# A one-core decoder trunk: second operand of the opening between two quarters of x, last k tile's weights ahead of its columns and split

## The chip, the cores and the metric

The kernel runs on one core of a Trainium2 chip. The metric is device time in microseconds (us), the median of several executions; lower is better. The engines are named as the profile names them: PE (matmul; PEld is its weight load), DVE (vector), ACT (scalar), POOL, and SP, whose queue issues most of the transfers.

## The reference, cut to what matters

Two residual layers over x (256 tokens by 2048), each a mixer and a SwiGLU feed-forward. Every sub-layer first normalises x and modulates it with a shift and a scale that are products of silu(c) with a large matrix:

```python
silu_c = jax.nn.silu(c)
for layer in range(DEPTH):
    mod = silu_c @ mod_w[layer] + mod_b[layer]
    sh1, sc1, g1, sh2, sc2, g2 = jnp.split(mod, 6, axis=-1)
    h = modulate(rms_norm(x, norm_mix_gain[layer]), sh1, sc1)
    ...                                  # proj = h @ w_in, first step of the mixer
```

For the opening this means: before the first projection can use row block k of `w_in` (128 of the 2048 inner values, a "k tile", 16 of them), the 128 shifts and 128 scales of that block must be known, and each takes a full row of `mod_w`: two tiles of 128x2048, 1 MB each.

## The kernel before, in words

The opening (`start`) works by k tiles, kt = 0 to 15. For each one SP fetches three 1 MB tiles: two of `mod_w` (`mod_s`, here called the columns of kt, `fetch_columns`) and one of the projection's first 2048 output columns (`raw_s`, its weights, `fetch_weights`). All 48 go through SP's one queue, in program order: an issue that waits for a buffer holds up all issues behind it. `rawp` has three buffers for weights (`RAWS`), so weights kt wait until weights kt-3 have been read.

- `columns(kt)`: DVE multiplies each of the two column tiles with `silu_c` and sums (`mod_sum`, L109), then two small operations (`column_factors`, L998 and L1000) make scale and shift.
- `operand(kt)`: ACT applies them to the turned x (`tm_s`, L1015), casts to fp32r (`hT_s` high part, L1016), and DVE makes the low part (L1017).
- `weights(kt)`: unless kt is in `PLAIN`, ACT casts the weights to a high part (`hi_s`, L167, two halves) and DVE subtracts to a low part (`lo_s`, L169, two halves).
- `products(kt)`: PE adds this k tile to eight accumulators of 128x512 (four groups of columns in the order 1, 3, 0, 2, two tiles of tokens). A split tile takes three fp32r matmuls for each (L1031 high by high, L1032 high by low weights, L1033 low by high), 24 in all; a plain tile takes one fp32 matmul for each (L1026), which the trace lists as two entries, 16 in all.

The loop body for kt issues the columns of kt+2, the weights of kt+1, then `columns(kt + 1)`, `weights(kt)`, `operand(kt + 1)` and `products(kt)`: on DVE the split of tile kt stands behind the sums of tile kt+1. Every instruction in `start` keeps its written order (`manual_schedule`). Ahead of the loop x itself is scaled and turned in four quarters of 512 columns (`scaled`, `turned`), and tile 0 is multiplied in two halves.

After the opening ACT reads accumulators 1 and 3 through SiLU into `qg_A` (L1113) and PE starts on the next projection pieces (`acc_A`, L190 to L192), whose accumulator is one that `qg_A` frees. The rest of the program is placed by a scheduler.

Of the kernel before, what the change touches and what calls it, by code (L numbers as in the profile page):

```python
# [18 lines left out]
KT = D // P  # L19
# [2 lines left out]
LOG_MIN_FORGET = float(np.log(np.float32(1e-30)))  # L22
LEVELS = (64, 32, 16, 8, 4, 2, 1)
FFN_GROUPS = ((0, 6), (6, 12), (12, 18), (18, 22))
PLAIN = (0, 3, 6, 9, 12, 15)
LOOKAHEAD = 2
RAWS = 3
HIS = 4
# [38 lines left out]
def build(tc, ctx, a, out):  # L67
# [9 lines left out]
    def ps_mix(name):  # L77
        return env["pm"].tile([P, 512], F32, tag="pm", name=name)

    def h_tile(name):  # L80
        return hpool.tile([P, 2, 4, T], F32R, tag="h", name=name)
# [26 lines left out]
    def mod_sum(tile, l, part, j):  # L108
        nc.vector.scalar_tensor_tensor(tile, tile, 1.0, silu_c, ALU.mult, ALU.mult,  # L109
                                       accum_out=modc[l, part][:, j:j + 1])  # L110
# [169 lines left out]
    def rsqrt(dst, ss, n, width, name, between=lambda: None):  # L280

        m = small.tile([P, width], F32, tag=f"rs_m{width}", name=f"rsm_{name}")
        u = small.tile([P, width], F32, tag=f"rs_u{width}", name=f"rsu_{name}")
        nc.vector.tensor_scalar(m, ss, 1.0 / n, EPS, ALU.mult, ALU.add)
        nc.scalar.activation(u, m, AF.Ln)
        nc.scalar.activation(dst, u, AF.Exp, scale=-0.5)
        between()
        nc.vector.scalar_tensor_tensor(u, dst, -0.5, dst, ALU.mult, ALU.mult)
        nc.vector.tensor_tensor(u, u, m, ALU.mult)
        nc.vector.scalar_tensor_tensor(dst, u, 1.5, dst, ALU.add, ALU.mult)  # L290
# [26 lines left out]
    def new_ss(name):  # L317
        return small.tile([P, 2, 4], F32, tag="ss", name=f"ss_{name}")
# [643 lines left out]
    def start():  # L962
# [13 lines left out]
        hT, raw_w, raw_m = [], {}, {}  # L976

        def fetch_columns(kt):
            for part in (1, 0):
                if (2 * kt + 1 - part) % 3 == 2:  # L980
                    tl = rawp.tile([P, D], F32, tag="modraw", name=f"mod_s{part}_{kt}", bufs=2)
                else:
                    tl = hpool.tile([P, D], F32, tag="h", name=f"mod_s{part}_{kt}")
                nc.sync.dma_start(out=tl, in_=a["mod_w"][0, part * KT + kt])
                raw_m[part, kt] = tl

        def fetch_weights(kt):
            raw_w[kt] = rawp.tile([P, 2048], F32, tag="raw", name=f"raw_s{kt}")
            nc.sync.dma_start(out=raw_w[kt], in_=a["start_w"][kt])

        def columns(kt):
            for part in (1, 0):
                mod_sum(raw_m[part, kt], 0, part, kt)
            column_factors(kt)

        def column_factors(kt):
            k = slice(kt, kt + 1)
            nc.vector.scalar_tensor_tensor(acol[:, k], modc[0, 1][:, k], b1[:, k], cols[:, C_NMIX + kt:C_NMIX + kt + 1],  # L998
                                           ALU.add, ALU.mult)
            nc.vector.tensor_tensor(modc[0, 0][:, k], modc[0, 0][:, k], cols[:, C_MODB + kt:C_MODB + kt + 1], ALU.add)  # L1000

        def weights(kt):
            if kt in PLAIN:
                return None
            return [split_weights(raw_w[kt][:, n * 1024:(n + 1) * 1024], f"s{kt}_{n}") for n in range(2)]
# [3 lines left out]
        def operand(kt):  # L1009
            if kt % 4 == 0:  # L1010
                hT.append(h_tile(f"hT_s{kt // 4}"))
            h = hT[-1]
            k = slice(kt, kt + 1)
            tm = tms[kt] = pool.tile([P, T], F32, tag="tm", name=f"tm_s{kt}", bufs=3)
            nc.scalar.activation(tm, xT[:, kt, :], AF.Identity, bias=modc[0, 0][:, k], scale=acol[:, k])  # L1015
            nc.scalar.copy(out=h[:, 0, kt % 4], in_=tm)  # L1016
            nc.vector.tensor_tensor(h[:, 1, kt % 4], tm, h[:, 0, kt % 4], ALU.subtract)  # L1017

        def products(kt, ws, ns):

            for n in ns:
                sl = slice((n % 2) * 512, (n % 2 + 1) * 512)
                for t in range(2):
                    o = acc[n][t]
                    if ws is None:
                        nc.tensor.matmul(o, tms[kt][:, t * P:(t + 1) * P], raw_w[kt][:, n * 512:(n + 1) * 512],  # L1026
                                         start=(kt == 0), stop=(kt == KT - 1))
                        continue
                    hi, lo = ws[n // 2]
                    a_hi, a_lo = act(kt, t)  # L1030
                    nc.tensor.matmul(o, a_hi, hi[:, sl], start=(kt == 0), stop=False)  # L1031
                    nc.tensor.matmul(o, a_hi, lo[:, sl], start=False, stop=False)  # L1032
                    nc.tensor.matmul(o, a_lo, hi[:, sl], start=False, stop=(kt == KT - 1))  # L1033

        def scaled(nb, t, engine):
            if engine is nc.scalar:
                nc.scalar.activation(xt[nb][:, t], xt[nb][:, t], AF.Copy, scale=r[:, t:t + 1])
            else:
                nc.vector.tensor_scalar(xt[nb][:, t], xt[nb][:, t], r[:, t:t + 1], None, ALU.mult)

        def turned(nb):
            for half in range(2):
                ps = ps_mix(f"xT_{nb}_{half}")
                for kk in range(2):
                    for t in range(2):
                        c0 = (half * 2 + kk) * P
                        nc.tensor.transpose(ps[:, kk * T + t * P:kk * T + (t + 1) * P], xt[nb][:, t, c0:c0 + P], ident)
                k0 = nb * 4 + half * 2
                nc.scalar.copy(out=xT[:, k0:k0 + 2, :].rearrange("p k t -> p (k t)"), in_=ps)

        fetch_columns(0)
        fetch_weights(0)
        fetch_columns(1)
        act = act_of(hT)
# [5 lines left out]
        with tc.tile_pool(name="ps_t", bufs=4, space=PSUM) as pt:  # L1060
            env["pm"] = pt
            ss = new_ss("s")
            nc.vector.tensor_scalar(b1, cols[:, C_MODB + KT:C_MODB + 2 * KT], 1.0, None, ALU.add)
            for nb in range(4):
                ps = ps_mix(f"c_{nb}")
                sl = slice(nb * 512, (nb + 1) * 512)
                nc.tensor.matmul(ps, ones, c_row[:, sl], start=True, stop=True)
                nc.scalar.activation(silu_c[:, sl], ps, AF.Silu)
                junk = [pool.tile([P, 512], F32, tag=f"junk{t}", name=f"junk_s{nb}{t}", bufs=1) for t in range(2)]
                nc.vector.scalar_tensor_tensor(junk[0], xt[nb][:, 0], 1.0, xt[nb][:, 0], ALU.mult, ALU.mult,  # L1070
                                               accum_out=ss[:, 0, nb:nb + 1])
                nc.scalar.activation(junk[1], xt[nb][:, 1], AF.Square, accum_out=ss[:, 1, nb:nb + 1])
            nc.scalar.preload_act_table_set(EXP_LN)
            tot = small.tile([P, 2], F32, tag="sst2", name="sst_s", bufs=1)
            r = small.tile([P, 2], F32, tag="rstd2", name="rstd_s", bufs=1)
            nc.vector.tensor_reduce(tot, ss, op=ALU.add, axis=AX.X)
            rsqrt(r, tot, D, 2, "s", lambda: mod_sum(raw_m[1, 0], 0, 1, 0))
            for t in range(2):
                scaled(0, t, nc.vector)
            turned(0)  # L1080
            mod_sum(raw_m[0, 0], 0, 0, 0)
            column_factors(0)
            operand(0)
            products(0, weights(0), (1, 3))
            for nb in range(1, 4):
                scaled(nb, 0, nc.scalar)
                scaled(nb, 1, nc.vector)
                turned(nb)
        env["pm"] = ctx.enter_context(tc.tile_pool(name="pm", bufs=4, space=PSUM))
        for u in range(2):  # L1090
            acc[2 * u] = [ps_mix(f"acc_s{u}_{t}") for t in range(2)]
        products(0, None, (0, 2))
        fetch_weights(1)
        columns(1)
        operand(1)
        fetch_columns(2)
        for kt in range(1, KT):
            if kt + 2 < KT:
                fetch_columns(kt + 2)
            if kt + 1 < KT:  # L1100
                fetch_weights(kt + 1)
                columns(kt + 1)
            if kt == 3:
                nc.scalar.preload_act_table_set(SILU)
            ws = weights(kt)
            if kt + 1 < KT:
                operand(kt + 1)
            products(kt, ws, (1, 3, 0, 2))
# [206 lines left out]
    with tc.manual_schedule():  # L1315
        started = start()
# [102 lines left out]
```

## Time and profile before

| | |
|---|---|
| median of 3 runs | 2498.66 us (2498.23 to 2498.86) |
| profiled execution, its own time | 2495.23 us |
| its span, first to last instruction | 2493.5 us |
| PE busy | 2442.0 us, 98% of the span |
| DVE busy | 1772.8 us, 71% |
| ACT busy | 1168.8 us, 47% |
| opening, to the last matmul on `acc_s` | about 147.5 us |

The profiled execution stands 3.43 us under the median of the runs, and its span 1.73 us under its own time. A change of the span is therefore added to the median as it is. All times in the text count from the start of the span.

### The profile page before, as it was taken

The page shows a single profiled execution, that of the slowest core. Times are in us where ns is not written, and L with a number is a line of the kernel's source. Part 1 is how long each engine was busy: PE and PEld are TensorE (multiplying, and loading weights), DVE is VectorE, ACT ScalarE, POOL GpSimd, SP SyncE. Part 2 cuts the span into 40 slices and gives each one's busy share as a digit, 9 for nine tenths or more (in the row PEclk, how much of TensorE's full clock was granted, in tenths as well). Part 3 has the DMA queues.
Part 4 walks back from the last instruction along what each step waited for, and adds up shares of the span by engine and source line. Part 5 has one row for each costly group of instructions (what it writes and reads, how often), then busy time and mean ns, then how long its engine had stood idle before and what let it go on. Part 6 is the DMA issues. An engine that isn't in the chain of part 4 may idle for free.

```text
span 2493.5 us, 28661 instructions
## 1 busy us (share of the span) xinstructions
PE 2442.0 (98%) x11204; PEld 2002.5 (80%) x11204; DVE 1772.8 (71%) x2039; ACT 1168.8 (47%) x1625; POOL 89.6 (4%) x176
## 2 busy tenths in 40 slices
PE   7899999999999999999999999999999999999999
PEld 4578887887888888888888888888888888888887
DVE  6967887887788767767767787876776554644555
ACT  4255555545434444344345666654544344344343
POOL 0000000000000000000000000000000000000000
PEclk9999999999999999999999999999999999999999
DMA  9964767985798877777786667677486555555554
GB/s 390 420 258 168 286 253 290 347 320 215 288 367 339 318 285 285 289 286 283 286 292 208 236 246 248 250 280 260 175 313 237 188 195 189 188 191 193 190 189 148
DMA packets 93849, 647.48 MB, mean 260 GB/s; under 512 B 10417, under 2 KB 10993, under 8 KB 16401
## 3 DMA queue, kind: packets, MB, share of 16 engines
q1 hardware_dynamic: 70290, 476.59, 52.4%
q0 software_dynamic: 23424, 169.07, 18.2%
q8 instruction: 87, 1.43, 0.2%
q14 instruction: 48, 0.39, 0.0%
HBM read 641.39 MB, written 4.23 MB: 259 GB/s over the span
## 4 chain that ended last, share of the span: by engine, by line
PE 93%; DVE 4%; DMA 2%; ACT 1%; issue 1%; SPq 0%; ACTq 0%
PE acc_F L192 13%; PE acc_F L190 13%; PE acc_F L191 13%; PE acc_G L190 6%; PE acc_G L192 6%; PE acc_G L191 6%; PE acc_C L192 4%; PE acc_C L190 4%; PE acc_C L191 4%; PE acc_B L190 2%; PE acc_B L192 2%; PE acc_B L191 2%; PE acc_O L190 2%; PE acc_O L192 2%; PE acc_O L191 2%; DMA raw_s<-in_start_w_dram 2%
## 5 line engine op out<-in xcount | busy, mean ns | idle before, releaser
L169 DVE TENSOR_TENSOR lo<-raw_F,hi 128x1024 fp32r<-128x1024 f32 x352 | 429.5, 1223 | 302.3 <-ACT hi L167 302.1
L167 ACT CAST hi<-raw_F 128x1024 fp32r<-128x1024 f32 x352 | 370.6, 1054 | 478.1 <-PE acc_F L192 433.2
L192 PE MATMUL acc_F<-hi,hT_f 128*128 128x512 f32 x1408 | 551.1, 391 | 1.4 <-DVE hT_f L357 1.4
L190 PE MATMUL acc_F<-hi,hT_f 128*128 128x512 f32 x1408 | 548.7, 390 | 1.8 <-ACT hT_f L356 1.8
L191 PE MATMUL acc_F<-lo,hT_f 128*128 128x512 f32 x1408 | 548.4, 390 | 0.0
L109 DVE SCALAR_TENSOR_TENSOR mod<-mod,silu_c 128x2048 f32<-128x2048 f32 x160 | 365.3, 2284 | 4.2 <-DMA mod<-in_mod_w_dram 4.2
L169 DVE TENSOR_TENSOR lo<-raw_G,hi 128x1024 fp32r<-128x1024 f32 x176 | 214.2, 1222 | 139.3 <-ACT hi L167 139.1
L167 ACT CAST hi<-raw_G 128x1024 fp32r<-128x1024 f32 x176 | 185.4, 1055 | 268.5 <-PE acc_G L192 227.3
L192 PEld LDWEIGHTS acc_F<-hi,hT_f 128*128 128x128 f32 x1408 | 264.4, 188 | 56.9 <-DVE hT_f L357 3.0
L190 PEld LDWEIGHTS acc_F<-hi,hT_f 128*128 128x128 f32 x1408 | 264.5, 188 | 55.8 <-ACT hT_f L356 2.2
L191 PEld LDWEIGHTS acc_F<-lo,hT_f 128*128 128x128 f32 x1408 | 264.3, 188 | 55.1
L190 PE MATMUL acc_G<-hi,ct_f 128*128 128x512 f32 x704 | 273.5, 389 | 1.6 <-DVE res_G L405 1.6
L192 PE MATMUL acc_G<-hi,ct_f 128*128 128x512 f32 x704 | 274.4, 390 | 0.0
L191 PE MATMUL acc_G<-lo,ct_f 128*128 128x512 f32 x704 | 273.7, 389 | 0.0
L190 PEld LDWEIGHTS acc_G<-hi,ct_f 128*128 128x128 f32 x704 | 132.2, 188 | 29.6 <-DVE res_G L405 2.4
L191 PEld LDWEIGHTS acc_G<-lo,ct_f 128*128 128x128 f32 x704 | 132.2, 188 | 27.4
L192 PEld LDWEIGHTS acc_G<-hi,ct_f 128*128 128x128 f32 x704 | 132.2, 188 | 27.2
L190 PE MATMUL acc_C<-hi,hT_n 128*128 128x512 f32 x384 | 152.4, 399 | 0.9 <-ACT hT_n L356 0.9
L192 PE MATMUL acc_C<-hi,hT_n 128*128 128x512 f32 x384 | 151.3, 394 | 0.7 <-DVE hT_n L357 0.7
L191 PE MATMUL acc_C<-lo,hT_n 128*128 128x512 f32 x384 | 151.7, 395 | 0.0
L104 POOL DMA_DIRECT2D mod<-in_mod_w_dram x160 | 84.5, 528 | 1612.8 <-DVE mod L109 1449.8
L169 DVE TENSOR_TENSOR lo<-raw_C,hi 128x1024 fp32r<-128x1024 f32 x96 | 116.1, 1220 | 35.2 <-ACT hi L167 34.8
(343 smaller groups left out, 3399.7 us busy)
## 6 DMA issues: line engine op xcount, KB each, us to landing
raw_F<-in_ffn_w_in_dram SPq DMA_DIRECT2D x176, 1024.0 KB, 4.9
mod<-in_mod_w_dram POOLq DMA_DIRECT2D x160, 1024.0 KB, 5.2
raw_G<-in_ffn_w_out_dram SPq DMA_DIRECT2D x88, 1024.0 KB, 4.9
raw_C<-in_gla_w_in_dram SPq DMA_DIRECT2D x48, 1024.0 KB, 5.6
mod_s<-in_mod_w_dram SPq DMA_DIRECT2D x32, 1024.0 KB, 17.0
raw_B<-in_ab_w_in_dram SPq DMA_DIRECT2D x32, 1024.0 KB, 6.6
raw_s<-in_start_w_dram SPq DMA_DIRECT2D x16, 1024.0 KB, 13.9
raw_A<-in_ab_w_in_dram SPq DMA_DIRECT2D x16, 1024.0 KB, 5.0
```

Source lines behind the costliest of these rows:

```text
L104: nc.gpsimd.dma_start(out=tile, in_=a["mod_w"][l, part * KT + j])
L109: nc.vector.scalar_tensor_tensor(tile, tile, 1.0, silu_c, ALU.mult, ALU.mult, accum_out=modc[l, part][:, j:j + 1])
L167: nc.scalar.copy(out=hi, in_=w)
L169: env["lo"] = nc.vector.tensor_tensor(lo, w, hi, ALU.subtract)
L190: nc.tensor.matmul(o, a_hi, w_hi, start=(kt == 0), stop=False)
L191: nc.tensor.matmul(o, a_hi, w_lo, start=False, stop=False)
L192: nc.tensor.matmul(o, a_lo, w_hi, start=False, stop=(kt == last))
```

## The change

The program has three edits in `start`. Tile 15 leaves `PLAIN`, so that its weights are split. `fetch_weights`, `columns` and `operand` of tile 1, and the fetch of columns 2, are written behind the second quarter of x (`nb == 1`) and no longer behind the fourth. And the weights of tile 15 are issued directly behind those of tile 14, with the columns of tile 15 behind both, where before the columns of 15 stood ahead of the weights of 14.

```diff
-PLAIN = (0, 3, 6, 9, 12, 15)
+PLAIN = (0, 3, 6, 9, 12)
...
         def fetch_weights(kt):
+            if kt in raw_w:
+                return
...
                 turned(nb)
+                if nb == 1:
+                    fetch_weights(1)
+                    columns(1)
+                    operand(1)
+                    fetch_columns(2)
...
         products(0, None, (0, 2))
-        fetch_weights(1)
-        columns(1)
-        operand(1)
-        fetch_columns(2)
         for kt in range(1, KT):
-            if kt + 2 < KT:
+            if kt + 2 < KT - 1:
                 fetch_columns(kt + 2)
             if kt + 1 < KT:
                 fetch_weights(kt + 1)
+                if kt + 2 == KT - 1:
+                    fetch_weights(KT - 1)
+                    fetch_columns(KT - 1)
                 columns(kt + 1)
```

On SP's queue, at the end of the opening, the program before has these rows (`raw_s_713`, `735` and `777` are the weights of tiles 13, 14 and 15, `mod_s_15` the columns of tile 15, `raw_A` the first weights behind the opening):

```order
L989 DMA raw_s_713<-in_start_w_dram 128x2048
L984 DMA mod_s_15_731<-in_mod_w_dram 128x2048
L984 DMA mod_s_15_733<-in_mod_w_dram 128x2048
L989 DMA raw_s_735<-in_start_w_dram 128x2048
L989 DMA raw_s_777<-in_start_w_dram 128x2048
L160 DMA raw_A_0_831<-in_ab_w_in_dram 128x2048
```

The changed program has at the same place (`raw_s_731` and `733` are now the weights of tiles 14 and 15):

```order
L991 DMA raw_s_713<-in_start_w_dram 128x2048
L991 DMA raw_s_731<-in_start_w_dram 128x2048
L991 DMA raw_s_733<-in_start_w_dram 128x2048
L984 DMA mod_s_15_735<-in_mod_w_dram 128x2048
L984 DMA mod_s_15_737<-in_mod_w_dram 128x2048
L160 DMA raw_A_0_855<-in_ab_w_in_dram 128x2048
```

The two column tiles have moved behind the two weight tiles; nothing else in the queue has moved there.

On DVE, at the same place, the changed program has these rows (sums of the columns of 15, factors, the split of tile 14, the low operand of 15, the split of tile 15, the first split of `raw_A`):

```order
L109 SCALAR_TENSOR_TENSOR mod_s_15_735,modc_1_83<-mod_s_15_735,silu_c 128x2048
L109 SCALAR_TENSOR_TENSOR mod_s_15_737,modc_0_82<-mod_s_15_737,silu_c 128x2048
L1000 SCALAR_TENSOR_TENSOR acol_s<-modc_1_83,b_115,cols 128x1
L1002 TENSOR_TENSOR modc_0_82<-modc_0_82,cols 128x1
L169 TENSOR_TENSOR lo_s_0_784<-raw_s_731,hi_s_0_783 128x1024
L169 TENSOR_TENSOR lo_s_1_788<-raw_s_731,hi_s_1_787 128x1024
L1019 TENSOR_TENSOR hT_s_680<-tm_s_791,hT_s_680 128x256
L169 TENSOR_TENSOR lo_s_0_820<-raw_s_733,hi_s_0_819 128x1024
L169 TENSOR_TENSOR lo_s_1_824<-raw_s_733,hi_s_1_823 128x1024
L169 TENSOR_TENSOR lo_858<-raw_A_0_855,hi_857 128x1024
```

Before, the first seven of these stood in the same order, with the split of `raw_A` directly behind them: the two splits of tile 15 are new, and the split of tile 14 still stands behind the sums of the columns of tile 15.

On ACT, while x is turned, the changed program has (`x_s` scales half a quarter, `xT` copies a turned piece, `tm_s_223` and the cast behind it are the operand of tile 1):

```order
L1051 COPY xT<-xT_0_205 128x512
L1051 COPY xT<-xT_1_211 128x512
L1017 ACTIVATE tm_s_223<-xT,modc_0_82,acol_s 128x256
L1018 CAST hT_s_194<-tm_s_223 128x256
L1039 ACTIVATE x_s<-x_s,rstd_s 128x512
L1051 COPY xT<-xT_0_233 128x512
L1051 COPY xT<-xT_1_239 128x512
L1039 ACTIVATE x_s<-x_s,rstd_s 128x512
```

Before, the two rows of tile 1's operand stood behind all copies of x; now the third and fourth quarter's scaling and copies stand behind them.

## Rows read from the trace of the kernel before

**Rows 1.** The page's first part: busy us, share of the span, instructions.

```profile
PE 2442.0 (98%) x11204; PEld 2002.5 (80%) x11204; DVE 1772.8 (71%) x2039; ACT 1168.8 (47%) x1625; POOL 89.6 (4%) x176
```

**Rows 2.** Busy time by stretch: length, PE, PEld, DVE, ACT, POOL; PEclk, DMA share, GB/s.

```profile
110.00:120.00 10.00, 10.00 (x34) 6.44 (x35) 8.64 (x11) 1.48 (x4) 0.53 (x1) 1.00 1.01 418
120.00:130.00 10.00, 6.48 (x17) 3.88 (x16) 7.45 (x10) 2.90 (x4) 2.16 (x5) 0.83 1.02 416
130.00:140.00 10.00, 8.68 (x37) 6.65 (x36) 6.21 (x9) 4.91 (x6) 0.00 (x0) 1.00 0.81 311
```

**Rows 3.** SP's queue by time: start, us, line, operation, tile (first operations of the lines).

```profile
106.11 2.54 SPq L984 DMA_DIRECT2D mod_s<-in_mod_w_dram  x2
111.04 11.63 SPq L989 DMA_DIRECT2D raw_s<-in_start_w_dram  x2
127.44 35.16 SPq L160 DMA_DIRECT2D raw_A<-in_ab_w_in_dram  x7
```

**Rows 4.** Transfers issued near 39.0, 108.2, 111.0, 122.3, 136.2: us to landing.

```profile
raw_s<-in_start_w_dram SPq DMA_DIRECT2D x1, 1024.0 KB, 7.3
...
mod_s<-in_mod_w_dram SPq DMA_DIRECT2D x1, 1024.0 KB, 21.1
...
raw_s<-in_start_w_dram SPq DMA_DIRECT2D x1, 1024.0 KB, 21.7
...
raw_s<-in_start_w_dram SPq DMA_DIRECT2D x1, 1024.0 KB, 12.9
...
raw_A<-in_ab_w_in_dram SPq DMA_DIRECT2D x1, 1024.0 KB, 5.1
```

**Rows 5.** DVE by time: start, us, operation, tiles, [idle before, releaser].

```profile
34.00 0.42 DVE L1017 TENSOR_TENSOR hT_s<-tm_s,hT_s 128x256 fp32r<-128x256 f32 x1 [6.79 <-ACT hT_s L1016]
...
85.14 2.28 DVE L109 SCALAR_TENSOR_TENSOR mod_s<-mod_s,silu_c 128x2048 f32<-128x2048 f32 x1
...
87.56 2.35 DVE L169 TENSOR_TENSOR lo_s<-raw_s,hi_s 128x1024 fp32r<-128x1024 f32 x2
...
133.89 2.36 DVE L169 TENSOR_TENSOR lo_s<-raw_s,hi_s 128x1024 fp32r<-128x1024 f32 x2 [1.51 <-ACT hi_s L167]
```

**Rows 6.** PE by time, tiles 12 to 15 and the first matmul behind.

```profile
115.29 7.03 PE L1026 MATMUL acc_s<-raw_s,tm_s 128*128 128x512 f32 x16
126.33 0.80 PE L1032 MATMUL acc_s<-lo_s,hT_s 128*128 128x512 f32 x1 [0.76 <-DVE lo_s L169]
...
132.96 0.39 PE L1033 MATMUL acc_s<-hi_s,hT_s 128*128 128x512 f32 x1
...
135.16 0.50 PE L1032 MATMUL acc_s<-lo_s,hT_s 128*128 128x512 f32 x1 [0.75 <-DVE lo_s L169]
135.50 0.40 PE L1033 MATMUL acc_s<-hi_s,hT_s 128*128 128x512 f32 x1
...
140.51 7.03 PE L1026 MATMUL acc_s<-raw_s,tm_s 128*128 128x512 f32 x16
148.65 0.50 PE L190 MATMUL acc_A<-hi,hT_s 128*128 128x512 f32 x1 [1.11 <-ACT qg_A L1113]
```

**Rows 7.** ACT by time, at the end of the opening.

```profile
132.81 2.00 ACT L167 CAST hi_s<-raw_s 128x1024 fp32r<-128x1024 f32 x2 [5.90 <-DMA raw_s<-in_start_w_dram]
...
147.58 1.94 ACT L1113 ACTIVATE qg_A<-acc_s 128x1024 f32<-128x1024 f32 x2 [4.09 <-PE acc_s L1026]
```

**Rows 8.** ACT by time, the operand of tile 1.

```profile
32.93 0.60 ACT L1015 ACTIVATE tm_s<-xT,modc,acol_s 128x256 f32<-128x256 f32 x1
33.57 0.40 ACT L1016 CAST hT_s<-tm_s 128x256 fp32r<-128x256 f32 x1
```

**Rows 9.** PE by time, behind its longest wait after the opening.

```profile
392.08 0.55 PE L190 MATMUL acc_B<-hi,hT_s 128*128 128x512 f32 x1 [4.07 <-DVE g_B L794]
...
395.83 0.39 PE L190 MATMUL acc_B<-hi,hT_s 128*128 128x512 f32 x1
```

**Rows 10.** PE's waits from 148 to 700 us, the longest group: us in total, times, longest.

```profile
PE acc_B L190 <- DVE g_B L794: 4.3, 2, 4.1
```

## The prediction

> **What bounds the kernel now.** First the page's busy times: PE 98% of the span [rows 1], so nearly all of the program goes at PE's pace, and whatever moves the end of the opening moves the end of the program by as much, unless a later wait swallows it. Then the stretches of the opening. From 110 to 130 us the DMA engines are full (share 1.01 and 1.02, 416 to 418 GB/s) while PE is busy only 6.48 of 10 us in the second stretch, and from 130 to 140 the share falls to 0.81 [rows 2]: the opening is bound by its transfers until the last tile has landed, and then by what is done after it.
>
> When do they land? SP issues the columns of 15 at 106.11 to 108.65 (the second one at about 108.2), the weights of 14 at 111.04, and the weights of 15 at 111.04 + 11.63 - 0.33 = 122.34 [rows 3]. With the time to landing of each [rows 4]: second column tile 108.2 + 21.1 = 129.3, weights 14 at 111.04 + 21.7 = 132.74, weights 15 at 122.34 + 12.9 = 135.24. They land in the order of issue, 2.5 to 3.4 us apart. ACT casts weights 14 at 132.81, 0.07 after landing [rows 7]; DVE's subtraction starts at 133.89; PE's first matmul on it at 135.16, the rest of tile 14 ends at 140.51, and the plain tile 15 takes 7.03 [rows 5, 6]. Then PE idles 1.11 and starts `acc_A` at 148.65 [rows 6], since `qg_A` starts only at 147.58, after PE's last matmul [rows 7], though accumulators 1 and 3 are done half a tile earlier.
>
> **The change, step by step.** *The early operand of tile 1.* ACT's two operations, 0.60 + 0.40 us [rows 8], and DVE's 0.42 now stand ahead of the third quarter's scaling, so x is turned about 1.25 us later (estimate: the 1.00, and DVE's low part behind it, less overlap). On the other side DVE loses a 6.79 us wait [rows 5] and reaches the next sums up to 4 us earlier. That gain I cost at nothing: the transfers hide it, since full queues and not DVE decide when tiles 11 to 15 land [rows 2]. The delay has a price only if the queue runs dry: weights 3 are issued near 39.0, behind tile 0's last reader, and land 7.3 us later, where a transfer into a nearly empty queue takes 5.1 [rows 4]. The cover is 7.3 - 5.1 = 2.2 us, of which 1.25 is used. Value 0; ends: 0 to +1 us.
>
> *The order of the last four tiles.* The bytes are the same, so the last of the four lands at 135.24 as before, but it is now the second column tile: the weights of 14 and 15 move ahead of it. Weights 15 still wait for tile 12's last plain matmul (115.29 + 7.03 = 122.32, [rows 6]), and the columns, issued at 106 to 109 before, now queue behind that, at about 122.7 and 123.1. The first `raw_A`, at 127.44, is not held up: its buffer comes free then, as before.
>
> Behind that landing stands more work than before. DVE can start the sum at 135.24 + 0.07 = 135.31. From the start of a second sum to the start of the subtraction behind it are 87.56 - 85.14 = 2.42 us [rows 5], so 137.73: the split of tile 14, whose weights have long been there, waits behind the sums of columns 15 on DVE. From there to PE's first matmul on the low weights 135.16 - 133.89 = 1.27 us [rows 5, 6]: 139.00, where before it was 135.16. So the wait moves 3.84 us out, from weights 14 to columns 15.
>
> *Tile 15 split.* Removed: one plain tile, 7.03 us. Added: two casts on ACT (2.00, [rows 7]), two subtractions on DVE (2.36, [rows 5]) and 24 matmuls. Tile 14's 23 matmuls from 135.16 to 140.51 take 5.35 us, of which the first takes 135.50 - 135.16 = 0.34 [rows 6], so 0.228 each; 24 take 5.46. The split lies beside PE's tile 14: DVE has tile 14's two halves done at about 140.1, the low operand at 140.5, tile 15's first half at 141.7, before PE comes to it at 144.35. So -1.57 us. A second saving: tile 15 no longer reads `tm_s` on PE, and `qg_A` can start when accumulator 1 is done, a quarter into tile 15; the 1.11 us of idle [rows 6] goes.
>
> *PE's clock.* PE ends tile 13 at 132.96 + 0.23 = 133.19, does one matmul of tile 14 on the high weights, and idles until 139.00: some 5.5 us. After a wait of 4.07 us later in the trace, the nine matmul spacings from 392.08 to 395.83 take 3.75 us [rows 9]; at tile 14's pace (0.34 + 8 x 0.228) they would take 2.16. Loss 1.6. Tile 13, after two waits, needs 133.19 - 126.33 = 6.86 us for what tile 14 does in 5.35: loss 1.51, with a mean granted clock of 0.83 in that stretch [rows 2, 6], part of it at 1.2 GHz. I take 1.55; ends 0 (the clock stays up) and 2.2 (estimate: 1.6 x 5.5 / 4.07, in proportion to the wait).
>
> *The sum.* 139.00 + 5.35 + 5.46 + 1.55 = 151.36 for the start of `acc_A`, against 148.65: +2.7 us. On the profiled execution that is 2495.23 + 2.7 = 2497.9; on the median 2498.66 + 2.7 = **2501.4 us**, 0.11% more.
>
> *The rest.* The scheduler places the attention part a little differently. Nothing is added there but two DVE subtractions already counted. PE's longest wait there is 4.3 us in two pieces [rows 10]. Bounds: that wait gone, or one like it more, -4.3 to +4.3; I take 0.
>
> A measurement of this kernel can tell about 0.2%, 5 us, from no change: 2493.7 to 2503.7.
>
> **The rivals.** *The clock stays up* (12 in 100): +1.15, 2499.8. Against it both rows of the clock.
>
> *The columns land early* (8 in 100). The landings are in order of issue for tiles issued at least 2 us apart [rows 3, 4]; the columns follow weights 15 by 0.4, and no row shows that. If the second column tile changes place with weights 15 it lands at 132.74, 2.5 us earlier: +0.2, 2498.9. The Trainium skill's page "DMA: Bandwidth & Descriptors", section "Two DMAs through the same engine are not ordered", says that nothing orders transfers across the 16 engines; by that rule this could be, while the rows found order each time.
>
> *The edit gives what it removes* (6 in 100): 1.57 + 1.11 = 2.7 us less, 2496.0. It needs tile 14's first low matmul at 135.16 as before, so the columns by 131.4; the landing times speak against it.
>
> *The queue runs dry, slower by over 0.2%* (8 in 100). The columns stand on SP behind weights 15, and these behind PE's tile 12. With weights 14 landed at about 126.7 (one place, 2.5 us, ahead of 129.3), weights 15 must be issued 5.1 - 2.5 = 2.6 us before, by 124.1; they are issued at 122.34. Each microsecond over the 1.8 of cover delays the columns by one. It decides when tile 12 ends 4 us late (2.3 more than my 2.7), as it would with more than half of it at 1.2 GHz; the clock of 1.00 from 110 to 120 [rows 2] speaks against it. Then 2503.7 and more, 2505 for a loss of 3.6 beyond the sum.
>
> *The attention part falls differently* (8 in 100): 5 slower by over 0.2%, about 2505, 3 faster, about 2493.5 (2501.4 less 4.3, and more waits gone beside it).
>
> **How the numbers follow.** My forecast has 58 in 100, with a range of its own of 2500.3 to 2502.9. With the rivals: faster 0.03, same 0.58 + 0.12 + 0.08 + 0.06 = 0.84, slower 0.13. The range from 2497.5 to 2504.5 takes in the clock's two ends, the early columns, a 2 us shift of the attention part either way and the small side of the dry queue; outside lie the full saving (6), the faster attention part (3) and some of the slower cases.
>
> **What would show it.** In the changed profile the last `mod_s` sum starts at about 135.3, DVE's split of tile 14 at 137.7 instead of 133.89, PE waits some 5.5 us for it and then shows matmuls spaced 0.43 for about 3 us, tile 15 takes 5.5 instead of 7.03, and `acc_A` starts at 151.4 without idle time. DVE's wait of 6.79 is gone and the share of DMA from 40 to 120 unchanged. The prediction is wrong if the DMA share falls below 1 before 130, if the columns land by 132, or if PE's waits behind 200 us change by more than 3.

## The result and the profile after

| | before | changed |
|---|---|---|
| median, same chip | 2497.90 us (20 executions) | 2502.73 us (20 executions) |
| profiled execution, its own time | 2495.23 us | 2501.36 us |
| its span | 2493.5 us | 2499.6 us |

The ratio is 1.002 with an interval of 1.0013 to 1.0027, so the changed kernel takes 4.8 us more; measured once more beside the experiments the ratio was 1.0019, 1.001 to 1.0028. The prediction was 2501.4, or 2.7 us more, with a range from 2497.5 to 2504.5. The time lies in the range, at the edge of what the prediction called no change; the direction is right, the size short by about 2 us. That the predicted time misses by 1.3 us only is in part luck: the 3 runs it was added to stood 0.8 above the median of the 20.

The opening first. The page's first part of the changed kernel, which answers to [rows 1], and its windows, which answer to [rows 2]:

```profile
PE 2444.9 (98%) x11212; PEld 2007.9 (80%) x11212; DVE 1776.7 (71%) x2041; ACT 1170.2 (47%) x1627; POOL 90.0 (4%) x176
```

```profile
110.00:120.00 10.00, 10.00 (x35) 6.42 (x35) 8.41 (x11) 1.30 (x3) 0.54 (x1) 1.00 1.01 418
120.00:130.00 10.00, 6.53 (x16) 3.90 (x15) 5.20 (x7) 4.79 (x6) 2.17 (x5) 0.83 1.02 412
130.00:140.00 10.00, 4.78 (x19) 3.62 (x18) 7.33 (x10) 2.46 (x4) 0.00 (x0) 0.82 0.56 228
140.00:150.00 10.00, 10.00 (x39) 8.05 (x39) 5.73 (x8) 4.55 (x5) 0.41 (x1) 0.84 0.62 216
```

Up to 130 the queue is as full and PE as busy as before; DVE's 7.45 falls to 5.20, since the first sum of the columns of 15, which began at 127.67 before, is not there yet. Between 130 and 140 PE's busy time falls from 8.68 to 4.78 us, and the granted clock to 0.82. SP's queue, answering to [rows 3], and the transfers issued between 122 and 124, with the time to landing, answering to [rows 4]:

```profile
103.33 19.14 SPq L991 DMA_DIRECT2D raw_s<-in_start_w_dram  x3
122.51 0.91 SPq L984 DMA_DIRECT2D mod_s<-in_mod_w_dram  x2
```

```profile
mod_s<-in_mod_w_dram SPq DMA_DIRECT2D x2, 1024.0 KB, 10.9
raw_s<-in_start_w_dram SPq DMA_DIRECT2D x1, 1024.0 KB, 7.0
```

The weights of 15 are issued at 103.33 + 19.14 - 0.33 = 122.1 to 122.5 (one issue takes 0.33) and land 7.0 us later; the two column tiles follow at once and land last. DVE and PE behind that landing (answering to [rows 5, 6]):

```profile
132.47 2.29 DVE L109 SCALAR_TENSOR_TENSOR mod_s<-mod_s,silu_c 128x2048 f32<-128x2048 f32 x1 [4.97 <-DMA mod_s<-in_mod_w_dram]
134.97 2.29 DVE L109 SCALAR_TENSOR_TENSOR mod_s<-mod_s,silu_c 128x2048 f32<-128x2048 f32 x1 [0.19 <-DMA mod_s<-in_mod_w_dram]
137.39 2.36 DVE L169 TENSOR_TENSOR lo_s<-raw_s,hi_s 128x1024 fp32r<-128x1024 f32 x2
```

```profile
138.66 0.80 PE L1034 MATMUL acc_s<-lo_s,hT_s 128*128 128x512 f32 x1 [5.22 <-DVE lo_s L169]
139.26 0.63 PE L1035 MATMUL acc_s<-hi_s,hT_s 128*128 128x512 f32 x1
139.68 0.63 PE L1033 MATMUL acc_s<-hi_s,hT_s 128*128 128x512 f32 x1
...
143.37 0.40 PE L1033 MATMUL acc_s<-hi_s,hT_s 128*128 128x512 f32 x1
...
146.10 0.39 PE L1033 MATMUL acc_s<-hi_s,hT_s 128*128 128x512 f32 x1
...
151.54 0.39 PE L190 MATMUL acc_A<-hi,hT_s 128*128 128x512 f32 x1
394.82 0.50 PE L190 MATMUL acc_B<-hi,hT_s 128*128 128x512 f32 x1 [4.07 <-DVE g_B L794]
```

The two sums wait for their transfers (4.97 and 0.19), the split of tile 14 follows at 137.39, and PE has waited 5.22 us for it. Its next matmuls stand 0.43 apart, those from 143.37 on 0.23 (24 of them fill 146.10 to 151.54): half clock, which is 1.2 GHz, for some 4.5 us. Tile 15 begins at 146.10 and `acc_A` at 151.54 without idle time, 2.89 behind before. The wait for `g_B` is 4.07 as before, and 394.82 - 392.08 = 2.74 later: from the opening to here nothing was added.

The second loss stands near 546. These are PE in the kernel before, then PE and ACT in the changed one:

```profile
535.15 0.38 PE L757 MATMUL sc_B<-qkTs_B 128*128 128x128 f32 x2
...
536.43 0.44 PE L190 MATMUL acc_O<-hi,ct_m 128*128 128x512 f32 x1
...
541.96 0.28 PE L781 MATMUL pT_B<-ident,s_B 128*128 128x128 f32 x1
...
546.33 0.50 PE L190 MATMUL acc_O<-hi,ct_m 128*128 128x512 f32 x1 [0.68 <-ACT ct_m L372]
```

```profile
540.84 0.38 PE L757 MATMUL sc_B<-qkTs_B 128*128 128x128 f32 x2
...
542.12 0.44 PE L191 MATMUL acc_O<-lo,ct_m 128*128 128x512 f32 x1
...
546.39 0.33 PE L781 MATMUL pT_B<-ident,s_B 128*128 128x128 f32 x1 [1.53 <-ACT s_B L775]
...
550.82 0.50 PE L190 MATMUL acc_O<-hi,ct_m 128*128 128x512 f32 x1 [0.68 <-ACT ct_m L372]
```

```profile
544.90 1.04 ACT L167 CAST hi<-raw_O 128x1024 fp32r<-128x1024 f32 x1 [1.66 <-PE acc_O L192]
545.85 0.40 ACT L775 ACTIVATE s_B<-s_B,mx_B 128x128 f32<-128x128 f32 x1
```

PE computes attention scores (`sc_B`), DVE and ACT make the softmax (`s_B`), PE turns it (`pT_B`). Before, 24 matmuls on `acc_O` stand between the scores and `pT_B` and cover the softmax; in the changed program 13 of them have moved ahead of the scores, 11 are left, and PE waits 1.53 us. The cast of the next weights that stands ahead of the exponential on ACT (544.90, then 545.85) stood there before too (540.11, then 541.07), so it is the cover that differs. Nobody wrote this: the scheduler, whose input is the opening's instructions too, placed the rest differently; from about 400 to 545 us PE's rows stand in another order. The second `acc_O` row is 4.49 behind before, so this place adds 4.49 - 2.74 = 1.75 us. Together 2.74 to 2.89 from the opening and 1.75 from here: 4.5 to 4.6 us, against 4.8 measured.

The spans of the two profiled executions differ by 6.1. What is beyond 4.6 is a fall of the clock near 608 in the one profile and not in the other, 1.6 us; the last experiment asks whether it belongs to the change.

### The profile page after: what moved, and what is told of

Its sections match the earlier page's. It is cut to its first block, busy times and chain, and to the rows that moved or that the text cites. A ratio compares the mean times of both kernels' runs of the same rounds, so it can differ in the third digit from the quotient of the medians.

```text
span 2499.6 us, 28682 instructions
## 1 busy us (share of the span) xinstructions
PE 2444.9 (98%) x11212; PEld 2007.9 (80%) x11212; DVE 1776.7 (71%) x2041; ACT 1170.2 (47%) x1627; POOL 90.0 (4%) x176
## 4 chain that ended last, share of the span: by engine, by line
PE 93%; DMA 3%; DVE 2%; ACT 1%; issue 0%; SPq 0%; ACTq 0%
PE acc_F L192 13%; PE acc_F L190 13%; PE acc_F L191 13%; PE acc_G L190 6%; PE acc_G L192 6%; PE acc_G L191 6%; PE acc_C L192 4%; PE acc_C L190 4%; PE acc_C L191 4%; PE acc_B L190 2%; PE acc_B L191 2%; PE acc_B L192 2%; PE acc_O L190 2%; PE acc_O L191 2%; PE acc_O L192 2%; DMA raw_s<-in_start_w_dram 2%
```

## The experiments

The theory: the early operand is worth nothing; the tail costs 2.9 us in the opening, by columns that now land behind the last weights; the order of the rest costs 1.75 us more. The rivals: the early operand delays x and costs something itself; the split costs later what it saves in the opening; the second loss comes from the opening's state and not from the order.

**The operand alone.** The kernel before, with the call for tile 1 between the quarters of x:

```diff
                 turned(nb)
+                if nb == 1:
+                    fetch_weights(1)
+                    columns(1)
+                    operand(1)
+                    fetch_columns(2)
```

> Only the early operand of tile 1 is taken over; the end of the opening is that of the kernel before, and so is the order of everything behind it. Theory (transfers set the pace, the early operand is worth nothing): acc_A starts at 148.6 us, DMA share stays at 1 until 130, ratio 1.000 within 0.001. Rival (the early operand is part of the loss, by a queue that runs dry or a later x): acc_A later by 1 us or more, up to 2.9.

Measured: 2497.75 us, ratio 0.9998 (0.9989 to 1.0007). Windows from 40 on and the end of the opening:

```profile
40.00:120.00 80.00, 73.76 (x254) 48.36 (x253) 72.61 (x93) 24.82 (x37) 0.54 (x1) 0.98 1.01 419
```

```profile
148.78 0.50 PE L190 MATMUL acc_A<-hi,hT_s 128*128 128x512 f32 x1 [1.11 <-ACT qg_A L1114]
```

DVE's wait of 6.79 is gone here too, and `acc_A` starts within 0.13 of before: the share of DMA is 1.01 all along, so the time won on DVE is spent waiting for transfers. The first edit is worth nothing that these runs can tell; the interval leaves about 2 us either way, `acc_A` 0.13.

**The tail alone.** The two other edits of the diff, on the kernel before.

> Only the end is taken over: weights 15 ahead of columns 15, tile 15 split; the operand of tile 1 stands where it stood. The order behind the opening is that of the changed kernel. Theory: acc_A at 151.5 us, the wait of PE on s_B of 1.5 us near 546, in all +4.6 us, ratio 1.002. Rival (the early operand carries part of the loss): acc_A at 149 to 150.5, ratio 1.001.

Measured: 2501.84 us, ratio 1.0017 (1.0008 to 1.0026). PE waits 5.33 us for the split of tile 14, `acc_A` starts at 151.11, and the wait on `s_B` is there:

```profile
138.23 0.79 PE L1034 MATMUL acc_s<-lo_s,hT_s 128*128 128x512 f32 x1 [5.33 <-DVE lo_s L169]
...
545.98 0.33 PE L781 MATMUL pT_B<-ident,s_B 128*128 128x128 f32 x1 [1.53 <-ACT s_B L775]
```

The wait on `s_B` and the opening's loss both come with the tail's two edits, and so does the whole loss, as far as the interval tells it from the changed kernel's 1.002.

**The order of transfers alone.** As above, but tile 15 stays plain:

```diff
 PLAIN = (0, 3, 6, 9, 12, 15)
...
-            if kt + 2 < KT:
+            if kt + 2 < KT - 1:
                 fetch_columns(kt + 2)
             if kt + 1 < KT:
                 fetch_weights(kt + 1)
+                if kt + 2 == KT - 1:
+                    fetch_weights(KT - 1)
+                    fetch_columns(KT - 1)
```

> The kernel before with only the order of the last four transfers changed (weights of 14 and 15 ahead of the columns of 15); tile 15 stays plain, tile 1's operand stays late. Theory: first low matmul of tile 14 near 138.7 behind a wait of 5.2, half clock for 3 us, tile 15 in 7.03, then the idle 1.1 before acc_A, which starts near 138.7 + 5.35 + 1.5 + 7.03 + 1.1 = 153.7, +5.0 against before; the wait of 1.53 on s_B near 548 is there too, since its order of the rest is nearly that of the changed kernel; total +5 to +7.5, ratio 1.002 to 1.003. Rival (the split costs as much as the plain tile): acc_A near 151.5 and the total as with the changed kernel, 1.0017 to 1.002.

Measured: 2507.37 us, ratio 1.0031 (1.0018 to 1.0043).

```profile
138.57 0.80 PE L1034 MATMUL acc_s<-lo_s,hT_s 128*128 128x512 f32 x1 [4.50 <-DVE lo_s L169]
...
146.74 7.03 PE L1028 MATMUL acc_s<-raw_s,tm_s 128*128 128x512 f32 x16
154.88 0.50 PE L190 MATMUL acc_A<-hi,hT_s 128*128 128x512 f32 x1 [1.11 <-ACT qg_A L1118]
```

The order alone costs 6.2 us in the opening, 1.2 more than expected (tile 14 took 8.17 us from 138.57, longer at half clock than in the changed kernel). Up to `acc_O` (555.35) it is 9.0: the wait on `s_B` is there, and half clock lasts longer behind the wait on `g_B` too. The total, 8.7 over before, lies above the 5 to 7.5 expected. The split gives 154.88 - 151.54 = 3.3 of the opening's loss back, of which 7.03 + 1.11 - 5.44 = 2.7 are its own rows and the rest is half clock in tile 14: the rival that the split is worthless falls.

**The split alone.** The kernel before, with one line changed:

```diff
-PLAIN = (0, 3, 6, 9, 12, 15)
+PLAIN = (0, 3, 6, 9, 12)
```

> Only tile 15 is split; the transfers keep their order. The order of the attention part is that of the changed kernel. Theory (the loss in the opening comes from the columns that land last, the split itself gains): first low matmul of tile 14 at 135.2, tile 15 in 5.5 us from 140.5, acc_A at 146.0, 2.7 earlier than before; the wait on s_B is there and takes 1.75 back; in all -1.0 us, ratio 0.9996. Rival (the split's work on ACT and DVE is what costs): acc_A at 148.6 or later.

Measured: 2507.70 us, ratio 1.0038 (1.0024 to 1.0052), 9.3 us over before, where a gain was expected. The opening did what it should, the rest did not; PE:

```profile
134.98 0.50 PE L1032 MATMUL acc_s<-lo_s,hT_s 128*128 128x512 f32 x1 [0.30 <-DVE lo_s L169]
...
145.78 0.39 PE L190 MATMUL acc_A<-hi,hT_s 128*128 128x512 f32 x1
...
328.01 0.80 PE L190 MATMUL acc_B<-hi,hT_s 128*128 128x512 f32 x1 [6.25 <-DVE g_B L794]
394.97 0.77 PE L558 MATMUL po_A<-v_A,st 128*128 128x128 f32 x2 [2.27 <-DVE st L548]
400.48 0.77 PE L190 MATMUL acc_B<-hi,hT_s 128*128 128x512 f32 x1 [3.89 <-DVE g_B L794]
552.65 0.33 PE L781 MATMUL pT_B<-ident,s_B 128*128 128x128 f32 x1 [1.53 <-ACT s_B L775]
```

`acc_A` is 2.87 ahead of before. Then stand a wait of 6.25 that before has nowhere, two waits on `po_A` and the one on `s_B`. The waits on `g_B`, `po_A` and `s_B` are 10.1 + 3.3 + 1.5 here against 4.3 before [rows 10], 10.6 more, and the clock falls behind them. The program's rows behind the opening stand in another order here than in the kernel before, and from 160 to 400 us in another than in the changed kernel too, whose order the expectation had assumed. Whether it is this order or the split itself that costs so much, the next run separates.

**The split, with the rest in the order of before.** A DVE copy of a constant (`lvl`) behind the opening is written five times instead of once. It changes no value; by it the scheduler puts all but some fifty rows of PE near the opening into the order of the kernel before.

```diff
-PLAIN = (0, 3, 6, 9, 12, 15)
+PLAIN = (0, 3, 6, 9, 12)
...
         nc.vector.tensor_copy(out=lvl, in_=lraw)
+        nc.vector.tensor_copy(out=lvl, in_=lraw)
+        nc.vector.tensor_copy(out=lvl, in_=lraw)
+        nc.vector.tensor_copy(out=lvl, in_=lraw)
+        nc.vector.tensor_copy(out=lvl, in_=lraw)
```

> The kernel before with tile 15 split, as in the run with only the split, and with one DVE copy of a constant (lvl, 0.75 us) behind the opening written five times instead of once; by that the scheduler puts the instructions behind the opening in the order of the kernel before, but for some fifty rows of PE near the opening. Theory (the opening pays what its rows say, the order of the rest costs the remainder): first low matmul of tile 14 at about 135.1, acc_A at about 145.8 as in the run with only the split, and then no wait of 6.25 on g_B near 328, none on po_A near 395 and none of 1.53 on s_B near 550; acc_O at 543.5 to 545 instead of 557; the total 2 to 2.9 us under the kernel before, a ratio near 0.999, in spite of 3 us more work on DVE. Rival (the split itself costs something later, by its weights, its buffers or the clock): the total stays near +9.5 us, ratio 1.0038, with acc_O near 557.

Measured: 2495.33 us, ratio 0.9986 (0.9977 to 0.9995). With the same split and more work on DVE it takes 12.4 us less than the split alone. The longest groups of PE's waits from 148 to 700:

```profile
PE acc_B L190 <- DVE g_B L794: 4.3, 2, 4.1
PE acc_A L190 <- ACT v_A L584: 1.5, 1, 1.5
```

They are those of before: no 6.25, no `po_A`, no `s_B`. `acc_A` stood at 147.62 in this profile, 1.8 later than expected, mostly because the clock fell during tile 14 (spacing 0.43 from 136.3 to 139.3), and `acc_O` at 545.71, where 545 at most was expected. The order of the rest is worth more than the edit in the opening.

**The changed kernel, with the old order behind.** The same means on the changed kernel, with eleven copies in place of one: the instructions behind about 300 us stand in the order of before, the opening stays.

> The changed kernel, with the DVE copy of the constant lvl written eleven times, by which the scheduler returns the instructions behind about 300 us to the order of the kernel before. The opening is untouched: acc_A at 151.5. The ten copies (6.7 us on DVE from 149 on, in its idle time of 3.4 and beside ACT's casts) may hold up PE near 155 by 0 to 3 us. Theory (the second part of the loss is the order near 546): no wait of 1.53 on s_B, and from acc_B's wait (near 394.8) to acc_O 154.3 us as before, not 156.0; the total is +2.9 and what the copies cost, +2.9 to +5. Rival (the 1.75 us come from the opening's state, the clock or the transfers, not from the order): 156.0 from acc_B to acc_O stays.

Measured: 2505.57 us, ratio 1.0027 (1.0017 to 1.0038). PE:

```profile
209.64 0.46 PE L558 MATMUL po_A<-v_A,st 128*128 128x128 f32 x2 [1.53 <-DVE st L548]
...
399.07 0.80 PE L190 MATMUL acc_B<-hi,hT_s 128*128 128x512 f32 x1 [4.07 <-DVE g_B L794]
...
549.05 0.33 PE L781 MATMUL pT_B<-ident,s_B 128*128 128x128 f32 x1
...
553.50 0.50 PE L190 MATMUL acc_O<-hi,ct_m 128*128 128x512 f32 x1 [0.68 <-ACT ct_m L372]
```

The total, 6.9 over before, misses the expectation: the ten copies, and the other order that they bring between 160 and 260 us, cost 4.25 us up to `acc_B` (a wait of 1.53 near 210 and half clock behind it), not 0 to 3. The question it was made for is answered all the same: the wait of 1.53 on `s_B` is gone, and from `acc_B` to `acc_O` it takes 553.50 - 399.07 = 154.43 us, as before (546.33 - 392.08 = 154.25) and not as in the changed kernel (156.00). The 1.75 us belong to the order.

**The split of tile 14 ahead of the columns.** The changed kernel, with DVE's work in the order in which it lands: the split of 14 ahead of the sums of columns 15, that of 15 behind them.

```diff
                     fetch_columns(KT - 1)
+                if kt + 2 == KT:
+                    ws = weights(kt)
                 columns(kt + 1)
...
-            ws = weights(kt)
+            if kt + 2 == KT:
+                last = weights(kt + 1)
+            else:
+                ws = last if kt + 1 == KT else weights(kt)
```

> The changed kernel, with the split of tile 14 ahead of the sums of columns 15 on DVE, and the split of tile 15 between these sums and the operand of 15; the transfers are those of the changed kernel. The attention part stands in the order of the kernel before. Theory (the order on DVE, not the landing of the columns, is what costs): tile 14 directly behind tile 13 at 133, tile 15 from 138.7 to 144.3, acc_A at 144.3, 4.3 us earlier than before, no wait on s_B; ratio 0.9983. Rival (the late columns cost by themselves): acc_A at 148.6 or later.

Measured: 2495.34 us, ratio 0.9986 (0.9977 to 0.9995) to the kernel before: 7 us under the changed kernel.

```profile
127.90 2.36 DVE L169 TENSOR_TENSOR lo_s<-raw_s,hi_s 128x1024 fp32r<-128x1024 f32 x2
132.75 2.29 DVE L109 SCALAR_TENSOR_TENSOR mod_s<-mod_s,silu_c 128x2048 f32<-128x2048 f32 x1 [2.49 <-DMA mod_s<-in_mod_w_dram]
135.23 2.29 DVE L109 SCALAR_TENSOR_TENSOR mod_s<-mod_s,silu_c 128x2048 f32<-128x2048 f32 x1 [0.18 <-DMA mod_s<-in_mod_w_dram]
...
137.65 2.35 DVE L169 TENSOR_TENSOR lo_s<-raw_s,hi_s 128x1024 fp32r<-128x1024 f32 x2
```

```profile
145.52 0.39 PE L190 MATMUL acc_A<-hi,hT_s 128*128 128x512 f32 x1
388.82 0.79 PE L190 MATMUL acc_B<-hi,hT_s 128*128 128x512 f32 x1 [4.07 <-DVE g_B L794]
544.28 0.50 PE L190 MATMUL acc_O<-hi,ct_m 128*128 128x512 f32 x1 [0.67 <-ACT ct_m L372]
```

The columns land when they did in the changed kernel, but tile 14 is split by 130.3 and PE works through their wait: none of its waits of 5 us is left, and `acc_A` starts 6.0 ahead of the changed kernel. It was expected at 144.3; half clock lasted in tile 13 until 132.0 here, until 129.7 in the kernel before. The scheduler happened to place the rest as before, so the gain arrives. Position on DVE, not the transfers' order as such, makes the loss in the opening. Nor does the new order of the transfers gain anything that shows: the split with the old order of transfers and of the rest measured the same 0.9986.

**The changed kernel again, and the kernel before twice more.** No edit; the question is what in one profile is the execution's.

> The changed kernel once more, without an edit, on the same chip as its neighbours. Theory: 4.6 us over before (2.9 from the opening, 1.75 from the wait on s_B and what goes with it), ratio 1.0013 to 1.0025, with the same two places in the trace; the half clock near 608 may be there or not, and its 1.6 us with it. Rival (the half clock near 608 belongs to the change): it is there again, and the span is 6 us over before.

Measured: 2502.80 us, ratio 1.0019 (1.001 to 1.0028). `acc_A` at 151.39, the wait of 1.53 at 546.21, 156.00 us from `acc_B` to `acc_O`: the same two places. The fall near 608 was there again, so it took the kernel before to judge it.

> The kernel before once more, one profile. In its first profile PE stayed at full clock behind the waits of 0.90 and 0.69 at acc_F (601 to 603), while the changed kernel fell to half clock there both times, which cost it 1.6 us of span. Theory (the fall there is a matter of the single execution): in one at least of two more profiles of the kernel before the granted clock between 600 and 615 is under 0.95. Rival (it goes with the later arrival of the changed kernel at that place): both stay at 1.00 there. The waits themselves are those of the first profile: 4.07 on g_B, none of 1.53 on s_B, acc_A at 148.3 to 149.2.

> The kernel before once more, a second profile of the same kind, with the same question and the same expectations as its neighbour: under 0.95 between 600 and 615 in one of the two by the theory, 1.00 in both by the rival.

The windows of 605 to 610, in the kernel before, in the changed one, and in the two further profiles of the kernel before:

```profile
605.00:610.00 5.00, 5.00 (x34) 4.53 (x33) 3.06 (x10) 1.82 (x6) 0.00 (x0) 1.00 0.00 0
```

```profile
605.00:610.00 5.00, 3.64 (x10) 2.60 (x10) 4.81 (x13) 4.57 (x13) 0.00 (x0) 0.74 0.76 279
```

```profile
605.00:610.00 5.00, 5.00 (x17) 3.99 (x16) 3.79 (x12) 3.19 (x9) 0.00 (x0) 0.69 0.36 149
```

```profile
605.00:610.00 5.00, 5.00 (x35) 4.57 (x34) 3.04 (x10) 1.80 (x5) 0.00 (x0) 1.00 0.00 0
```

The same program fell to 0.69 in one execution (span 2497.0 us) and stayed at 1.00 in the other (2493.7): the rival as it was put falls, and the 1.6 us can come without the change. Their waits are those of the first profile, with `acc_A` at 148.20 and 148.40. The profile of before on which the prediction rested was one of those without the fall. Whether the change makes the fall likelier stays open. The execution of before that fell reached this place later: its wait of 0.69 ended at 604.45, against 602.56 and 602.32 in the other two, after longer half clock behind `g_B` and a fall near 547. Of the twelve profiles of this case the clock fell here in all seven whose wait of 0.69 ended after 604, the two of the changed kernel among them, and in one of the five where it ended earlier. From `acc_B` to `acc_O`, the distance from which the 1.75 was read, it is 154.25, 154.92 and 154.28 us in the three profiles of before and 156.00 in both of the changed kernel.

## Why the prediction was right, and where it was short

*The early operand, 0.* Right: 0.9998 alone, and the queue at 1.01 to 1.02 with and without it. The last piece of x was copied at 33.59 instead of 32.45, 1.14 later for 1.25 estimated, and the 2.2 us of cover were enough.

*The columns land last.* Right: 135.31 was predicted for the last sum, 134.97 measured; the split at 137.73, measured 137.39; the first low matmul at 139.00, measured 138.66. The rival that the columns overtake the last weights did not happen. The Trainium skill's page "DMA: Bandwidth & Descriptors", section "Two DMAs through the same engine are not ordered", says that nothing orders transfers across the 16 engines. In the six profiles of kernels that issue the two column tiles behind the last weights, the last sum started between 134.54 and 135.28 every time, where the rival had the second column tile landed at 132.74; so the overtaking did not happen here, and no run shows that it cannot.

*Tile 15 split.* Right: 146.10 to 151.54, 5.44 against 5.46 predicted, and `acc_A` without the idle 1.11.

*PE's clock, 1.55.* A little small. Tile 14's 23 matmuls took 146.10 - 138.66 = 7.44 us against 5.35 at full clock, a loss of 2.09, near the upper end of 2.2 that was scaled from the wait's length. Behind the same columns it was 2.36 in the changed kernel's second profile, 2.09 with the tail alone and 1.62 with the old order behind, 1.6 to 2.4 in four profiles: the mechanism was right and 1.55 the low end of what it costs. The 0.54 of this profile and the 0.34 by which the landing was early leave the opening at +2.89 for +2.7.

*The rest, 0.* This step failed. It was set to 0 with ends of 4.3 either way, because nothing was added there; measured is +1.75, from a wait of 1.53 on `s_B` that before did not have. It is the rival "the attention part falls differently", which had 8 in 100, arriving beside the forecast and not in its place. The trace of before could not show it, but the order of the changed program has 13 matmuls moved ahead of the scores. With the 24 that the trace of before has between scores and `pT_B`, and 11 left of them, the lost cover of 13 x 0.228 = 3.0 us could have been priced, the most that the wait can grow if the way from scores to `pT_B` takes no longer. The run with only the split shows how large this term can be: about 12 us for an edit of 2.9.

## What to carry to other kernels

When part of a program is placed by a scheduler, an edit anywhere ahead of it can change the order far behind, and that may weigh more than the edit: look for the matmuls that stand between a producer and the consumer that waits for it, in both orders, and price the cover that is lost. Before a variant is judged by its total, compare the distance between two marks behind the edit. And an engine that takes its work in the written order, as DVE does in this opening, wants it in the order in which the data lands: moving a transfer back cost 6 us up to `acc_A` here while other work stood behind its reader, and nothing once that work was moved ahead of it.

## What the hardware showed that was not expected

The granted clock behind the same two short waits (0.90 and 0.69 us) fell to 0.69 in one execution and stayed at 1.00 in another of the same program, and that kernel's 20 executions spread over 2494.56 to 2502.12 us. A wait of 5.22 us in the opening was followed by some 4.5 us at half clock, a loss of 2.09, against 1.6 behind 4.07; behind the same 4.07 one further execution of the kernel before lost 2.2 (eleven spacings in 4.85 us, from 391.65 to 396.50). Behind 4.50 in the run with only the order changed half clock lasted from 138.57 to 144.3, a loss of 2.8, and in the split with the order of before the clock fell in tile 14 with no wait over 0.76 just ahead of it. So the length of the wait alone did not set the loss.
